# A decoder layer in float32 on one core: half-size weight buffers, the second FFN's weight sums added from DRAM to DRAM during the attention, seven sums kept on chip, token sums in the opening

## The chip, the cores and the metric

The kernel runs on one core of a Trainium2 chip. The time is the device time of one execution in microseconds (us); the number that counts is the median of several runs. A profile of one execution stands beside the times: it lists every instruction of the engines TensorE (PE, and PEld for its weight loads), VectorE (DVE), ScalarE (ACT), GpSimd (POOL) and SyncE (SP), and the DMA transfers.

## The reference

One decoder layer for 512 tokens of width 1024, in float32: a half-step SwiGLU FFN, a token mixer, and a second half-step FFN, each inside RMSNorms.

```python
x = x + 0.5 * rms_norm(swiglu(rms_norm(x, ffn1_pre), w_gate1, w_up1, w_down1), ffn1_post)
y = token_mixer(rms_norm(x, mix_pre), ...)     # sparse + dilated attention, gated, projected
x = x + rms_norm(y, mix_post)
x = x + 0.5 * rms_norm(swiglu(rms_norm(x, ffn2_pre), w_gate2, w_up2, w_down2), ffn2_post)
# swiglu(h, g, u, d) = (silu(h @ g) * (h @ u)) @ d,   d_ff = 2816
```

The mixer projects to queries, keys and values of two attentions. The first ("nsa": 8 heads, each with a selected and a window branch, so 16 head items, plus compressed keys) and the second ("dil": dilated windows, 12 heads) are weighed with gates and projected back.

## The kernel before

**Numbers.** Every float32 operand is split into a high part (ScalarE, a cast that rounds) and a low part (VectorE, the difference), in `split`, L102. A product is three matmuls: high x high, low x high, high x low (`mm3`, L124).

**FFN, gate and up.** The 2816 hidden rows are 11 pairs of 128-row blocks (even and odd). For each pair the gate and up weights are four blocks of 512 KB, by input half h and member f. The first two pairs (`PLAIN`) are computed plainly. The other nine pairs use a Winograd form of Strassen's scheme: seven half-width products P1 to P7 instead of eight, with sums of weights (VectorE, `prep`, L429) and sums of tokens T1 to T4 (`token_sums`, L510). Their order is P2, P6, P5, P7, the next pair's P1, P4, P3 (`todo`, L495), and the weights of a product are prepared two products ahead (`AHEAD`). The weights come through three buffers called raw of 1 MB, each holding one (pair, h), loaded by SP (`load`, L281): the first half of the next pair after P2 is prepared, the second after P7.

**Sums of activations.** After each pair, `sums` (L343) forms the sums that the down product needs. One (E) is split and stays; X, the odd block (O) and Y are stored to DRAM by SP (`sxdram`, `odram`, `ydram`) and read back in the down product, four reloads ahead (`STAGED`), into slots named SP.

**Sums of down weights (the table).** The down product uses the same seven-product form with half as many tokens. Four of its seven weight operands are sums of quarters of the down weight: T2, T4, T1, T3. GpSimd's DMA queue makes them, in both FFNs, beside the gate and up work (`weight_sums`, L308): per block of 256 KB it loads two quarters into SBUF slots named PT, adds others with an accumulating DMA (`accum_op`), and stores the sums into a DRAM tile `tdram`. The steps are put behind the work of given pairs by a list (`SUMS`, L34), with a one-column copy on GpSimd that waits for the pair (L363).

**FFN, down.** `ffn_down` (L556) runs seven products in the order B11, T2, T3, T1, B21, B22, T4. Each reads its weights in three loads of up to 1 MB through the raw buffers, and between them splits the reloaded X, O and Y.

**Opening.** `opening` (L1436) runs the first pair for the first FFN with an order of instructions written by hand on ScalarE, VectorE and TensorE. The normalisation is applied afterwards, by a row of factors (`row`, L1507), so the squares of x (L1495), the power on GpSimd (L1497), a diagonal (L1500) and a matmul with ones (L1506) make that row. After it x transposed is multiplied by its gain (L1510), and the token sums are formed from it after the first pair, on VectorE (L521). T4 is copied into the place of a part of the tokens before the first seven-product pair (L413 to L418).

**Attention.** In `nsa` (L1043) each of the 16 head items has its scores, its softmax, a scaling of the probabilities by GpSimd (L1008) and ScalarE (L1006), transposes (L1017) and the value product, the last three two items later (`LAG`). Pieces of the gate projection fill in between (`merge_unit`).

**Order.** Outside the opening a scheduler orders each engine's queue from the program's order and the dependencies; `issue_after` adds an order between two instructions of one engine. Each queue, SP's and GpSimd's DMA issues too, is first in, first out: an instruction that waits holds all behind it.

Of the kernel before, what the change touches and what calls it, by code (L numbers as in the profile page):

```python
# [12 lines left out]
F32 = mybir.dt.float32  # L13
F32R = mybir.dt.float32r
# [18 lines left out]
STAGED = 4  # L33
SUMS = [(0,), (1, 2)] + [(p + 1,) for p in range(2, 9)] + [(10, 11, 12), ()]  # L34
# [22 lines left out]
class Layer:  # L57
# [214 lines left out]
    def ffn(self, gu, wd, post, finish, xsrc, aside=None, opened=None):  # L272
# [5 lines left out]
        raws = {}  # L278
        later = {}

        def load(p, h):  # L281
            if (p, h) not in raws and p < NP:
                raws[p, h] = self.raw(gu[h, p].rearrange("p (f c) -> p f c", f=2), [2, D])

        def blk(p, h, f):
            return raws[p, h][:, f]
# [21 lines left out]
        def weight_sums(p):  # L308
# [3 lines left out]
            part = lambda q, e, h: wd[(2 * q + e) * P:(2 * q + e + 1) * P, h * S:(h + 1) * S]  # L312
# [12 lines left out]
            if one:  # L325
                put(self.tdram[p - 1][:, 0], later[p - 1][0])
            if two:
                put(self.tdram[p - 2][:, 1], later[p - 2][0])
            if new:
                for e in range(2):  # L330
                    put(self.tdram[p][:, 2 + e], r[e])
# [3 lines left out]
        E = []  # L335

# [6 lines left out]
        def sums(p, ev, od):  # L343

            h = slice(0, 256), slice(256, 512)
            x, y = self.slot("CB"), self.slot("ring")
# [5 lines left out]
            nc.sync.dma_start(self.sxdram[p], x)  # L352
# [5 lines left out]
        def extra(p):  # L358
            if p == 4 and aside:
                aside()  # L360
            if SUMS[p]:
                mark = self.sbt("mark", [P, 1])
                behind = nc.gpsimd.tensor_copy(mark, E[p][0][:, 0:1].bitcast(F32)).ins  # L363
                with self.tc.issue_after(behind):
                    for q in SUMS[p]:
                        weight_sums(q)

        banks = dict(opened["banks"]) if opened else {}
        if opened:
            raws.update(opened["raws"])  # L370
        else:
            ents = []
            for f in range(2):
                for h in range(2):
                    load(0, h)
                    w = entry(blk(0, h, f), len(ents) == 3)
                    ents.append(w)
# [11 lines left out]
        tops = None  # L389
        for p in range(PLAIN):  # L390
            acts = []
            for h in range(2):
                load(p + 1, h)
            for f in range(2):
                key = 2 * p + f
                if p:
                    ws = [None if (key, 0) in banks and h == 0 else entry(blk(p, h, f)) for h in range(2)]
# [11 lines left out]
            if p == 0:  # L409
                tops = self.token_sums(t_tags, opened)  # L410
            extra(p)
        t4 = tops["T4"]
        for m, v in enumerate((self.xht, self.xlt)):  # L413
            dst = v[:, 0:4, 256:512]
            if m == 0:
                nc.scalar.copy(dst, t4)
            else:
                nc.vector.tensor_sub(dst, t4, self.xht[:, 0:4, 256:512].bitcast(F32))  # L418
# [10 lines left out]
        def prep(p, name):  # L429
            st = state.setdefault(p, {})  # L430
            if name == "P1":
                load(p, 0)
                load(p, 1)
# [11 lines left out]
            elif name == "P7":  # L445
                src = blk(p, 0, 1)
                nc.vector.tensor_sub(src, blk(p, 0, 0), src)
# [57 lines left out]
        self.ffn_down(E, wd, post, finish, xsrc, opened)  # L505
# [4 lines left out]
    def token_sums(self, tags, opened):  # L510
# [4 lines left out]
        if opened:  # L515
            xt = opened["xt"]

        def diff(dst, a, b):
            if opened:
                for j in range(4):  # L520
                    nc.vector.tensor_sub(dst[:, j], xt[a[0] + j][:, a[1]], b[:, j] if not isinstance(b, tuple) else xt[b[0] + j][:, b[1]])  # L521
                return
# [10 lines left out]
        def keep(name, t):  # L533
            parts = [], []
            for m in range(2):
                w = [self.slot(tags.pop(0), F32R).rearrange("p (j c) -> p j c", j=2) for _ in range(2)]
                self.split(w[0], w[1], t[:, 2 * m:2 * m + 2])
# [1047 lines left out]
```

## Time and profile before

| what | us |
|---|---|
| median of 3 runs (lowest, highest) | 1189.32 (1188.61, 1190.68) |
| the profiled execution | 1193.05 |
| its span, first to last instruction | 1191.1 |

The stages as they lie in the span: opening and first FFN from 0 to about 375 us, the first attention's heads from about 430 to 555, the second attention and the projections to about 830, the second FFN from there to the end. In the profile a row of an engine list gives the start and length in us, engine, line, operation, operand shapes, and in brackets the idle time before it with what ended it. A row of the table of windows gives the busy time and the count of instructions of each engine, the granted TensorE clock as a share, the share in which the 16 DMA engines were busy, and GB/s.

### The profile page before, as it was taken

How to read it: one execution, taken by the hardware profiler on the slowest of the kernel's cores; microseconds unless marked ns; L12 is line 12 of the kernel's file. 1: busy time of each engine (PE TensorE's matmuls, PEld its weight loads, DVE VectorE, ACT ScalarE, POOL GpSimd, SP SyncE). 2: the span in 40 equal slices, each digit the busy share in tenths (PEclk: the TensorE clock that was granted, in tenths of full speed). 3: DMA queues.
4: the chain of work that ended last, by engine and by line, in shares of the span. 5: the costliest groups of instructions: out<-in, count | busy, mean ns of one | idle time of the engine just before them, and what ended most of it. 6: DMA issues, size and time to landing. Idle time of an engine off the chain costs nothing.

```text
span 1191.1 us, 18466 instructions
## 1 busy us (share of the span) xinstructions
PE 1138.5 (96%) x6863; PEld 1001.6 (84%) x6863; DVE 881.2 (74%) x1553; ACT 641.5 (54%) x1154; POOL 245.4 (21%) x350
## 2 busy tenths in 40 slices
PE   9899999978999999999999999999998999978997
PEld 7699999966877988778888898888898999976885
DVE  5789899957668779687444647966977898856675
ACT  5645455546455677686564625544443555535552
POOL 1143324230002032343000000001243333330001
PEclk9999999989999999999999999999998999998999
DMA  9598999999856462111224516473279998999863
GB/s 334 178 250 240 232 270 265 275 304 325 301 195 181 117 175 80 49 50 47 79 79 125 160 57 182 140 248 137 89 222 236 282 263 259 256 308 325 310 203 128
DMA packets 126859, 236.97 MB, mean 199 GB/s; under 512 B 22033, under 2 KB 51761, under 8 KB 121393
## 3 DMA queue, kind: packets, MB, share of 16 engines
q1 hardware_dynamic: 103392, 177.84, 45.4%
q0 software_dynamic: 23232, 57.69, 20.0%
q8 instruction: 54, 0.88, 0.3%
q14 instruction: 37, 0.30, 0.1%
q10 hardware_dynamic: 144, 0.26, 0.1%
HBM read 187.73 MB, written 48.02 MB: 198 GB/s over the span
## 4 chain that ended last, share of the span: by engine, by line
PE 52%; DVE 18%; DMA 13%; issue 10%; ACT 4%; POOL 1%; SPq 0%; DVEq 0%; POOLq 0%; ACTq 0%
PE pb_F L128 7%; PE pb_F L127 7%; PE pb_F L126 7%; DMA raw<-in_gu_dram 7%; DVE wlo L104 5%; PE pb_S L128 4%; PE pb_S L127 4%; PE pb_S L126 4%; PE pb_T L127 3%; PE pb_T L128 3%; PE pb_T L126 3%; DMA PT_s<-in_ffn_w_down_dram 3%; PE pb_V L1032 2%; DMA raw<-in_ffn_w_down_dram 1%; PE pb_T L1017 1%
## 5 line engine op out<-in xcount | busy, mean ns | idle before, releaser
L104 DVE TENSOR_TENSOR wlo<-raw,whi 128x1024 fp32r<-128x1024 f32 (+2 forms) x237 | 280.3, 1186 | 173.4 <-ACT whi L103 166.7
L103 ACT CAST whi<-raw 128x1024 fp32r<-128x1024 f32 (+2 forms) x237 | 241.1, 1018 | 268.1 <-PE pb_F L127 56.6
L126 PE MATMUL pb_F<-xh_t,whi 128*128 128x512 f32 (+1 forms) x440 | 156.7, 356 | 1.9 <-DVE Q_s L1242 1.1
L128 PE MATMUL pb_F<-xh_t,wlo 128*128 128x512 f32 (+1 forms) x440 | 155.7, 354 | 1.2 <-DVE wlo L104 1.2
L127 PE MATMUL pb_F<-xl_t,whi 128*128 128x512 f32 (+1 forms) x440 | 155.5, 353 | 0.0
L311 POOL DMA_DIRECT2D PT_s<-in_ffn_w_down_dram x88 | 78.4, 997 | 100.1 <-DMA PT_s<-in_ffn_w_down_dram 69.4
L126 PEld LDWEIGHTS pb_F<-xh_t,whi 128*128 128x128 f32 x440 | 82.9, 188 | 13.1 <-DVE Q_s L1242 1.3
L128 PEld LDWEIGHTS pb_F<-xh_t,wlo 128*128 128x128 f32 x440 | 82.9, 188 | 12.9 <-DVE wlo L104 2.2
L127 PEld LDWEIGHTS pb_F<-xl_t,whi 128*128 128x128 f32 x440 | 82.9, 188 | 11.0 <-issue 0.2
L128 PE MATMUL pb_S<-xh_t,wlo 128*128 128x256 f32 (+1 forms) x280 | 86.4, 309 | 4.5 <-DVE wlo L104 4.5
L126 PE MATMUL pb_S<-xh_t,whi 128*128 128x256 f32 (+1 forms) x280 | 86.6, 309 | 4.2 <-DVE V_s L482 3.8
L147 POOL TENSOR_TENSOR rs_t<-rs_t,mhalf_t 128x1 f32<-128x1 f32 x20 | 15.3, 763 | 358.4 <-DVE rs_t L143 358.4
L127 PE MATMUL pb_S<-xl_t,whi 128*128 128x256 f32 (+1 forms) x280 | 86.1, 307 | 0.0
L1008 POOL TENSOR_SCALAR SP_s<-SP_s,st_t 128x384 f32<-128x384 f32 (+2 forms) x48 | 47.8, 1012 | 103.9 <-DVE st_t L944 71.7
L126 PEld LDWEIGHTS pb_S<-xh_t,whi 128*128 128x128 f32 x280 | 55.0, 196 | 7.2 <-DVE V_s L482 4.0
L128 PEld LDWEIGHTS pb_S<-xh_t,wlo 128*128 128x128 f32 x280 | 54.9, 196 | 7.2 <-DVE wlo L104 5.0
L128 PE MATMUL pb_T<-xh_t,wlo 128*128 128x256 f32 x200 | 56.4, 282 | 1.1 <-DVE wlo L104 1.1
L127 PEld LDWEIGHTS pb_S<-xl_t,whi 128*128 128x128 f32 x280 | 55.0, 196 | 2.2
L126 PE MATMUL pb_T<-xh_t,whi 128*128 128x256 f32 x200 | 56.3, 282 | 0.0
L127 PE MATMUL pb_T<-xl_t,whi 128*128 128x256 f32 x200 | 56.1, 280 | 0.0
L103 ACT CAST whi<-tmp_t 128x1024 fp32r<-128x1024 f32 x36 | 37.6, 1048 | 21.1 <-issue 10.1
L128 PE MATMUL pb_S<-SP_s,wlo 128*128 128x256 f32 x160 | 45.4, 284 | 0.0
(799 smaller groups left out, 3322.3 us busy)
## 6 DMA issues: line engine op xcount, KB each, us to landing
raw<-in_gu_dram SPq DMA_DIRECT2D x42, 1024.0 KB, 7.2
PT_s<-in_ffn_w_down_dram POOLq DMA_DIRECT2D x132, 256.0 KB, 6.9
tdram<-PT_s POOLq DMA_DIRECT2D x88, 256.0 KB, 7.1
raw<-in_w_in_dram SPq DMA_DIRECT2D x18, 1024.0 KB, 5.5
raw<-tdram SPq DMA_DIRECT2D x16, 1024.0 KB, 7.4
raw<-in_ffn_w_down_dram SPq DMA_DIRECT2D x12, 1024.0 KB, 7.2
raw<-tdram SPq DMA_DIRECT2D x8, 768.0 KB, 6.7
odram<-W_s SPq DMA_DIRECT2D x22, 256.0 KB, 6.1
```

The costliest lines, as they stand in the source:

```text
L103: self.last_cast = self.nc.scalar.copy(dsthi, src).ins
L104: self.nc.vector.tensor_sub(dstlo, src, dsthi.bitcast(F32))
L126: mm(out, lhi, rhi, start=start, stop=False, skip_group_check=skip)
L127: mm(out, lhi, rlo, start=False, stop=False, skip_group_check=skip)
L128: mm(out, llo, rhi, start=False, stop=stop, skip_group_check=skip)
L147: nc.gpsimd.tensor_tensor(out=r, in0=v, in1=self.mhalf, op=OP.pow)
L311: add = lambda dst, src: put(dst, src, accum_op=OP.add)
L1008: nc.gpsimd.tensor_scalar(pp, pp, st[:, 1, t:t + 1], None, op0=OP.mult)
L1017: nc.tensor.transpose(b[:, o + (t - kk) * P:o + (t - kk + 1) * P], pt[pn][:, po + kk * P:po + (kk + 1) * P], self.ident)
L1032: self.nc.tensor.matmul(out[:, kk * P:S], v, pp, start=first and kk == 0 and pi == 0, stop=False, skip_group_check=True)
```

## The change

- **Weight buffers.** The three raw buffers are used as six halves of 512 KB. `ring_of` and `refill` load the blocks in their order of use; each half is refilled as soon as its block is used. P7's difference is formed while P6 is prepared. The weights lie in DRAM by blocks of 512 KB.
- **The first FFN's table** starts behind the row of the opening with two steps, and every later step comes one pair earlier; behind the pair of index 9 stand the steps 11 and 12, no longer 10.
- **The second FFN's table** is made in the first attention: `table_sums`, called for each of the 16 head items behind its scalings on GpSimd, copies and adds up to three blocks at a time from DRAM to DRAM; nothing passes SBUF. Its calls 0 to 13 hold 16 copies and 16 adds. Each FFN has its own `tdram`, and down weight and table lie in DRAM so that a partition's blocks are next to each other (a load's rows are 8 KB long).
- **Sums kept.** In the second FFN the X of the pairs from index 4 on (seven) stays in PT slots; it isn't stored and reloaded. Eight reloads are staged ahead instead of four.
- **Token sums.** In the first FFN they are formed in the opening, from x transposed, with the gain applied in the difference (`scaled_sums`); only four of the eight multiplications by the gain are left, ahead of the row. T4's split is in two halves.

The diff, cut to its core:

```diff
-STAGED = 4
-SUMS = [(0,), (1, 2)] + [(p + 1,) for p in range(2, 9)] + [(10, 11, 12), ()]
+STAGED = 8
+KEEP = 4
+SUMS = [(0, 1)] + [(p,) for p in range(2, 11)] + [(11, 12), ()]
...
+    def ring_of(self, gu, tiles, loaded):
+        self.order = [(h, p, f) for p in range(NF // 2) for f in range(2) for h in range(2)][loaded:]
+        self.blocks_of = {}
+        self.gu = gu
+        for t in tiles:
+            for f in range(2):
+                self.refill(t[:, f])
+
+    def refill(self, v):
+        if self.order:
+            key = self.order.pop(0)
+            self.nc.sync.dma_start(v, self.gu[key])
+            self.blocks_of[key] = v
...
-            x, y = self.slot("CB"), self.slot("ring")
+            x, y = self.slot("CB" if opened or p < KEEP else "PT"), self.slot("ring")
...
-            nc.sync.dma_start(self.sxdram[p], x)
+            if opened or p < KEEP:
+                nc.sync.dma_start(self.sxdram[p], x)
+            else:
+                kept[p] = x
...
+            if opened:
+                sums_behind(E[p][0][:, 0:1].bitcast(F32), SUMS[p + 1])
...
+            tops = opened["tops"]
+            sums_behind(row[:, 0:1], SUMS[0])
...
-                nc.vector.tensor_sub(src, blk(p, 0, 0), src)
...
-            if name == "P2":
-                load(p + 1, 0)
-            elif name == "P7":
-                load(p + 1, 1)
+            if name == "P6":
+                nc.vector.tensor_sub(blk(p, 0, 1), blk(p, 0, 0), blk(p, 0, 1))
+                self.refill(blk(p, 0, 0))
+            elif name in ("P7", "P4", "P3"):
+                self.refill(src)
...
+    def scaled_sums(self, tags, xt, g, out):
...
+        def diff(k, c, b):
+            t = new()
+            for j in range(4):
+                nc.vector.scalar_tensor_tensor(t[j // 2][:, j % 2], xt[k + j][:, c], g[:, k + j:k + j + 1], b(j),
+                                               op0=OP.mult, op1=OP.subtract)
+            return t
...
+        out["T3"] = self.keep_sum(tags, diff(4, hi, lambda j: xt[j][:, hi]))
+        t1 = less(lambda j: xt[j][:, hi], lambda j: xt[j][:, lo])
+        out["T1"] = self.keep_sum(tags, t1)
+        yield
+        t2 = diff(4, hi, of(t1))
+        out["T2"] = self.keep_sum(tags, t2)
+        out["T4"] = diff(4, lo, of(t2))
+        yield
...
             if m >= 0:
                 i, half, br = heads[m]
+                with self.tc.issue_after(self.last_pool):
+                    sums(m)
...
+    def table_sums(self, wd, td, call):
+        put = self.nc.gpsimd.dma_start
+        for b in range(0, NF // 2, 3):
+            q = slice(b, min(b + 3, NF // 2))
+            step = call - b
+            if step in (0, 1):
+                for i, e, h in ((2, 0, 1), (3, 1, 1), (0, 1, 1), (1, 1, 0))[2 * step:2 * step + 2]:
+                    put(td[i, :, q], wd[e, h, :, q])
+            elif step == 2:
+                put(td[2, :, q], wd[0, 0, :, q], accum_op=OP.add)
+                put(td[3, :, q], wd[0, 1, :, q], accum_op=OP.add)
+            elif step == 3:
+                put(td[0, :, q], td[2, :, q], accum_op=OP.add)
+            elif step == 4:
+                put(td[1, :, q], td[0, :, q], accum_op=OP.add)
...
             for t in range(NT):
                 if t == 2:
-                    w = self.wsplit(raws[1, 0][:, 0], [D])
+                    w = self.wsplit(third[:, 0], [D])
+                    self.refill(third[:, 0])
+                    for k in range(4):
+                        nc.scalar.mul(xt[k], xt[k], gcol[:, k:k + 1])
                 nc.scalar.activation(xn[t], xn[t], AF.Square, scale=D ** -0.5, accum_out=ss[:, t:t + 1])
+            tops = {}
+            sums = self.scaled_sums(list(T_TAGS), xt, gcol, tops)
+            next(sums)
             nc.vector.tensor_scalar(ss, ss, EPS, None, op0=OP.add)
             nc.gpsimd.tensor_tensor(out=rs, in0=ss, in1=self.mhalf.to_broadcast([P, NT]), op=OP.pow)
+            next(sums)
...
-            for k in range(KT):
-                nc.scalar.mul(xt[k], xt[k], gcol[:, k:k + 1])
...
-        self.tdram = self.tc.dram_tile([NF // 2, P, 4, S], F32, name="tdram")
+        td = [self.tc.dram_tile([4, P, NP, S], F32, name=f"tdram{i}") for i in range(2)]
...
+        self.mixer(*boundary(a["mix_post"][0], a["ffn2_pre"][0], self.x2dram, AFTER_MIX),
+                   lambda m: self.table_sums(a["d2"], td[1], m))
```

More of the change, by code (lines that the diff above doesn't have):

```diff
@@ L388, in ffn, with entered @@
                         mms(ents[2 * f + h], h, n, banks[f, n], 2 * P, S)
-        tops = None
+        def entered(p, h, f):
+            w = entry(blk(p, h, f))
+            self.refill(blk(p, h, f))
+            return w
         for p in range(PLAIN):
             acts = []
-            for h in range(2):
-                load(p + 1, h)
             for f in range(2):
@@ L396, in ffn @@
                 if p:
-                    ws = [None if (key, 0) in banks and h == 0 else entry(blk(p, h, f)) for h in range(2)]
+                    ws = [None if (key, 0) in banks and h == 0 else entered(p, h, f) for h in range(2)]
                     bs = [banks[key, n] if (key, n) in banks else self.bank() for n in range(2)]
@@ L408, in ffn @@
             sums(p, *acts)
-            if p == 0:
-                tops = self.token_sums(t_tags, opened)
+            if p == 0 and not opened:
+                tops = self.token_sums(t_tags)
             extra(p)
         t4 = tops["T4"]
[L413 to L418, printed above, removed]
+        for m in range(len(t4)):
+            n = 4 // len(t4)
+            c = slice(m * n, m * n + n), slice(256, 512)
+            self.split(self.xht[:, c[0], c[1]], self.xlt[:, c[0], c[1]], t4[m])
         tops.update(T4=self.xop(0, 256), B11=self.xop(0, 0), B21=self.xop(4, 0), B22=self.xop(4, 256))
@@ L504, in ffn, with keep_sum, token_sums @@
             finished(p, name)
-        self.ffn_down(E, wd, post, finish, xsrc, opened)
+        self.ffn_down(E, kept, wd, td, post, finish, xsrc, opened)
     def xop(self, k, c):
         return [lambda j, v=v: v[k + j][:, c:c + 256] for v in (self.xh, self.xl)]
-    def token_sums(self, tags, opened):
+    def keep_sum(self, tags, parts):
+        out = [], []
+        for t in parts:
+            w = [self.slot(tags.pop(0), F32R).rearrange("p (j c) -> p j c", j=2) for _ in range(2)]
+            self.split(w[0], w[1], t)
+            for o, v in zip(out, w):
+                o.append(v)
+        return [lambda j, v=v: v[j // 2][:, j % 2] for v in out]
+    def token_sums(self, tags):
         nc = self.nc
@@ L533, in keep @@
         def keep(name, t):
[L534 to L537, printed above, removed]
-                for o, v in zip(parts, w):
-                    o.append(v)
-            out[name] = [lambda j, v=v: v[j // 2][:, j % 2] for v in parts]
+            out[name] = self.keep_sum(tags, [t[:, 0:2], t[:, 2:4]])
         new = lambda: self.sbt("tmp", [P, 4, 256], bufs=2)
@@ L568, in ffn_down @@
         parts = {"X": [], "O": [], "Y": []}
-        srcs = [("X", i) for i in range(NP)] + [("O", i) for i in range(NP)] + [("Y", i) for i in range((NP + 1) // 2)]
+        srcs = [("X", i) for i in range(NP) if i not in kept] + [("O", i) for i in range(NP)] + [("Y", i) for i in range((NP + 1) // 2)]
         staged = {}
@@ L1440, in opening @@
         xt = [self.slot("x") for _ in range(KT)]
-        raw = [self.pool.tile([P, 4, S], F32, name="raw", tag="raw", bufs=3) for _ in range(2)]
+        raw = [self.raw_tile([4, S]) for _ in range(2)]
         gcol = self.sbt("gcol", [P, KT])
@@ L1456, in opening, with rows @@
         xn = []
-        raws = {}
-        for t in range(NT):
+        def rows(t):
             xn.append(self.sbt("tmp", [P, D], bufs=2))
             nc.sync.dma_start(xn[t], a["x"][0][t * P:(t + 1) * P])
-            if t % 2:
-                raws[1, t // 2] = self.raw(gu[t // 2, 1].rearrange("p (f c) -> p f c", f=2), [2, D])
+        self.ring_of(gu, (), 4)
+        third = self.raw_tile([2, D])
+        for t in range(2):
+            rows(t)
+            self.refill(third[:, t])
         ones = self.sbt("onesq", [P, P])
@@ L1487, in opening @@
                 nc.vector.tensor_sub(lo, src, hi.bitcast(F32))
+                if k % 2:
+                    self.refill(raw[k // 4].rearrange("p (a b) s -> p a (b s)", a=2)[:, (k // 2) % 2])
+                    if k < 4:
+                        rows(2 + k // 2)
                 for i, (l, r) in enumerate(((hi, xh[k]), (hi, xl[k]), (lo, xh[k]))):
```

95 lines of the change are left out of this document (49 added, 46 removed).

## The prediction

> **What bounds the kernel now.** I read the page first, then the table of stages (busy times in chosen windows), then the order-of-time lists of the engines around each hole, then the chain that ended last. The page gives the frame:
>
> ```profile
> span 1191.1 us, 18466 instructions
> ...
> PE 1138.5 (96%) x6863; PEld 1001.6 (84%) x6863; DVE 881.2 (74%) x1553; ACT 641.5 (54%) x1154; POOL 245.4 (21%) x350
> ...
> q1 hardware_dynamic: 103392, 177.84, 45.4%
> q0 software_dynamic: 23232, 57.69, 20.0%
> ```
>
> TensorE is the bound: 52.6 us idle in 1191.1. Idle time is not the whole loss, because matmuls after a hole run at a lower granted clock. So I count matmuls per window; the columns are busy time and (count) per engine, then granted clock, DMA share and GB/s.
>
> ```profile
> core 0: us, PE busy (x) PEld busy (x) DVE busy (x) ACT busy (x) POOL busy (x), PEclk, DMA share, GB/s
> 54.30:64.20 9.90, 5.75 (x29) 5.55 (x28) 9.87 (x15) 2.06 (x3) 4.08 (x7) 0.66 0.91 213
> 75.00:150.00 75.00, 71.67 (x581) 70.69 (x581) 66.61 (x92) 36.84 (x53) 25.32 (x38) 0.98 0.90 246
> 150.00:225.00 75.00, 75.00 (x635) 75.00 (x635) 71.72 (x102) 40.98 (x57) 25.68 (x39) 1.00 0.91 268
> 250.00:300.00 50.00, 39.75 (x149) 30.09 (x148) 32.26 (x44) 26.54 (x40) 6.15 (x10) 0.90 1.00 326
> 300.00:350.00 50.00, 49.93 (x217) 40.26 (x216) 30.87 (x36) 25.82 (x36) 0.00 (x0) 1.00 0.76 260
> 438.00:545.00 107.00, 106.09 (x592) 84.58 (x591) 88.12 (x274) 81.38 (x202) 42.84 (x48) 1.00 0.21 62
> ...
> 905.00:925.00 20.00, 15.84 (x110) 15.34 (x109) 13.39 (x18) 7.04 (x11) 5.97 (x9) 0.83 0.87 249
> ...
> 975.00:1050.00 75.00, 74.47 (x627) 74.06 (x626) 66.92 (x88) 39.44 (x58) 26.64 (x43) 1.00 0.95 266
> ...
> 1064.00:1100.00 36.00, 25.18 (x85) 18.62 (x84) 20.54 (x29) 18.38 (x28) 4.89 (x7) 0.81 1.00 324
> ```
>
> 150 to 225 is the undisturbed rate of the half-width products (635 in 75 us, 0.1181 us each), 300 to 350 that of the down product (217 in 50 us, 0.2304 each). What the other windows lose against these: 54.3 to 64.2: 9.9 - 29 x 0.1181 = 6.5 us; 75 to 150: 75 - 581 x 0.1181 = 6.4; 250 to 300: 50 - 149 x 0.2304 = 15.7; 905 to 925: 7.0; 975 to 1050: 0.9; 1064 to 1100: 16.4. Together 52.9 us, all in the two FFNs, and all but the first where the DMA share is 0.87 to 1.01. The attention (438 to 545) loses nothing and has the DMA engines at 0.21. The losses end on these transfers and queue entries:
>
> ```profile
> 132.86 8.34 DMA raw<-in_gu_dram
> ...
> 145.77 1.14 DVE raw L447
> ...
> 275.07 8.87 DMA PT_s<-in_ffn_w_down_dram
> ...
> 1051.39 17.24 DMA raw<-in_ffn_w_down_dram
> ...
> 1072.67 8.24 DMA sxdram<-CB_s
> ```
>
> ```profile
> 900.64 10.71 DMA raw<-in_gu_dram
> ```
>
> ```profile
> 259.41 0.79 PE L126 MATMUL pb_F<-whi,KB_s 128*128 128x512 f32 x1 [5.87 <-ACT whi L103]
> ```
>
> ```profile
> 1063.15 0.37 SPq L87 DMA_DIRECT2D raw<-tdram  x1
> ...
> 1083.55 0.37 SPq L87 DMA_DIRECT2D raw<-tdram  x1
> ```
>
> A down-weight load took 17.24 us. In the second down product, SP's queue went 20 us from one table load to the next (1063.15, 1083.55), because between them stands the reload of the last spilled X sum, which waits for its store (8.24 us from 1072.67).
>
> **Prices of the DMA work.**
>
> ```profile
> L311 POOL DMA_DIRECT2D PT_s<-in_ffn_w_down_dram x88 | 78.4, 997 | 100.1 <-DMA PT_s<-in_ffn_w_down_dram 69.4
> ...
> PT_s<-in_ffn_w_down_dram POOLq DMA_DIRECT2D x132, 256.0 KB, 6.9
> tdram<-PT_s POOLq DMA_DIRECT2D x88, 256.0 KB, 7.1
> raw<-in_w_in_dram SPq DMA_DIRECT2D x18, 1024.0 KB, 5.5
> ```
>
> q1 moves 177.84 MB in 45.4% of 1191.1 us: 0.329 MB/us, so a plain block of 256 KB (0.262 MB) takes 0.80 us of all 16 engines. q0 carries nothing but the table sums, 220 blocks, in 20.0%: 238 us. 132 of these are plain (105 us at 0.80), so the 88 adds (L311) take the other 133: 1.51 us each, nearly twice a plain one. One FFN's table (44 adds, 66 plain) costs 119 us of the DMA engines.
>
> **The change part by part.**
>
> *Token sums to the opening.* Now they stand on VectorE between the two plain pairs and the products:
>
> ```profile
> 40.30 2.77 DVE L521 TENSOR_TENSOR tmp_t<-x_s 128x256 f32<-128x256 f32 x8 [0.19 <-ACT x_s L1510]
> ...
> 45.93 0.68 DVE L104 TENSOR_TENSOR SP_s<-tmp_t,SP_s 128x512 fp32r<-128x512 f32 x1
> ...
> 55.96 1.21 DVE L418 TENSOR_TENSOR xl_t<-tmp_t,xh_t 128x1024 fp32r<-128x1024 f32 x1
> ...
> 57.43 1.22 DVE L104 TENSOR_TENSOR wlo<-raw,whi 128x1024 fp32r<-128x1024 f32 x1
> ```
>
> ```profile
> 58.70 0.58 PE L128 MATMUL pb_S<-xh_t,wlo 128*128 128x256 f32 x1 [4.15 <-DVE wlo L104]
> ```
>
> P1's weight split (57.43) comes last of a backlog, and TensorE waits 4.15 us and then runs at a granted clock of 0.66 in the window: the 6.5 us. The change takes 16 differences (2.77 / 8 = 0.35 each, 5.5 us) and six splits (0.68, 4.1 us) out of 40 to 54. The sum T4 is ready early, so its cast waits only for TensorE; L418 remains, as two halves of the same elements. I take the whole 6.5 as gone. The opening pays:
>
> ```profile
> 25.00 1.06 ACT L1495 ACTIVATE tmp_t<-tmp_t 128x1024 f32<-128x1024 f32 x1 [2.33 <-DMA tmp_t<-in_x_dram]
> ```
>
> ```profile
> 26.18 0.17 DVE L1496 TENSOR_SCALAR ssum_t<-ssum_t 128x4 f32<-128x4 f32 x1 [3.68 <-ACT tmp_t L1495]
> ...
> 36.60 1.23 DVE L104 TENSOR_TENSOR wlo<-raw,whi 128x1024 fp32r<-128x1024 f32 x1 [5.09 <-PE pb_V L1506]
> ```
>
> ```profile
> 35.55 1.02 PE L1506 MATMUL pb_V<-W_s,onesq_t 128*128 128x512 f32 x2
> ```
>
> T3's and T1's casts queue on ScalarE behind the last Square (26.1). In the written order four splits (2.7 us), four differences (1.4) and a cast's wait come ahead of L1496, which moves from 26.2 to about 30.7; then eight differences (2.8), two splits (1.4) and a cast come ahead of the diagonal. L1506 can start at 36 to 38 instead of 35.55. VectorE's 3.68 and 5.09 us of idle time cover the rest. I charge 2 us (0 to 4): net 4.5 gained (1 to 6.5).
>
> *Half-size buffers.* Bytes stay. A block's successor is asked for as soon as that block is used (P6, P7, P4, P3), nearly a pair (about 20 us) ahead of its use, where now the second 1 MB load of a pair goes out at P7, four products (4 x 24 x 0.118 = 11 us) ahead of it. The loads that end the chain take 8.34 and 10.71 us, so the longer lead covers them. P7's difference (1.14 us, L447) now stands in front of P5's split; preparation runs two products (5.7 us) ahead, which hides it; uncovered it would cost 1.1 us in each of nine pairs. I take 4.5 of the 6.4 us in the first FFN (0 to 6.4): there the DMA share stays at 0.91 and VectorE is 71.72 of 75 us busy.
>
> *First FFN's table one pair earlier.* Behind the last products now stand three steps of the table (10, 11, 12), then two (11, 12). Step 10 has 4 adds and 6 plain blocks: 4 x 1.51 + 6 x 0.80 = 10.8 us of DMA less in 250 to 300, paid from the 37 to 60 us stretch. On the other side STAGED 8 puts four more 256 KB reloads (3.2 us) ahead of the down loads, and the last two of the first product's three loads go into tiles free only at P3. Net 7.6 of the 15.7 us, and the down loads now read whole 8 KB rows; I take 9 (2 to 15).
>
> *Second FFN.* Its table leaves: 119 us of DMA time out of about 220 us that are 0.83 to 1.01 full, leaving a share near 0.45. The 10.71 us load goes back towards the 5.5 us of a quiet 1 MB load. I take 7.0 and 0.9 whole: 8 (6 to 8). Seven of the eleven X sums stay in SBUF, so the reload that blocked SP is gone, with 14 blocks. Of the 16.4 us I take 14 (9 to 16.4): the first product still has loads that wait for P3's tile.
>
> *The table in the attention.* 44 plain blocks and 44 adds, up to three blocks in a transfer: 35 + 66 = 101 us of DMA; with the 0.21 x 107 = 22 us already there, 123 us in the 107 us of the 14 calls. So the transfers lag, by up to 16 us at the end. Each add waits on POOL for the landing of the step before. Behind it on POOL stand the next head's probability scalings (L1008) and the key memsets of the dilated part; the transposes on TensorE (L1017) wait for the scalings. How much lag is free:
>
> ```profile
> 482.33 2.72 POOL L1008 TENSOR_SCALAR SP_s<-SP_s,st_t 128x384 f32<-128x384 f32 x3 [0.76 <-DVE st_t L944]
> ...
> 542.43 2.73 POOL L1008 TENSOR_SCALAR SP_s<-SP_s,st_t 128x384 f32<-128x384 f32 x3 [1.09 <-DVE st_t L944]
> ```
>
> ```profile
> 508.54 0.90 PE pb_T L1017 x8
> ...
> 550.18 0.76 PE pb_T L1017 x7
> ```
>
> In mid-attention the scalings are done 23 us before their transposes (485.1, 508.5), at the end 5 (545.2, 550.2). Issuing costs POOL about 1 us each (997 ns in the L311 row), two or three per head, against 42.84 of 107 us busy: free. I charge half of the lag, 8 us (0, as the middle heads' spare covers it all, to 20: the whole lag and two weight loads late by 2 us). An add between two DRAM places is not in the trace; its bounds are the plain block, 0.80, and twice the SBUF add, 3.0 (it may read both operands from DRAM); I take 1.51, the nearest row.
>
> The Trainium skill (DMA: Bandwidth & Descriptors, Anatomy of one DMA) fits a POOL-issued transfer as 2.0 us plus bytes / 436e3, with no extra term for adding. By it, an estimate, the 88 blocks move in 53 us and the attention pays nothing. The q0 row disagrees: 57.69 MB in 238 us is 0.242 MB/us.
>
> **Sum.** 4.5 + 4.5 + 9 + 8 + 14 - 8 = 32 us. The profiled execution took 1193.05 us (span 1191.1 and 1.95 around it): 1161. It stands 3.7 above the 1189.32 median of the three runs: 1157.
>
> **Rivals.**
> 1. *The adds are slow in DRAM; slower than before.* At x us a block, the calls need 22 + 35 + 44x us of DMA. Gains elsewhere are 40 us; with 8 us of lag absorbed, the sign turns at 107 + 48 = 155, x = 2.2. At x = 3.0 it is 189: 82 - 8 - 40 = 34 slower, 1223. For: 123 is already over 107. Against: source and destination streams both exist in the SBUF add at 1.51. Chance 0.07.
> 2. *DMA keeps the pace in the first FFN.* Its bytes are the same and only move by a pair; then its 13.5 us of stalls stay and the gain is 18.5: 1171. For: share 0.90 to 1.00 from 75 to 300. Chance 0.2.
> 3. *Adds cost no more than plain blocks, or the spare covers the lag.* 88 x 0.80 + 22 = 92 us fit in 107; nothing is charged: 1149; with the first FFN's holes nearly closed too (6.4 + 15.7 instead of 13.5), 1141. Against: the q0 row. The Trainium skill's fit quoted above (DMA: Bandwidth & Descriptors) would end here too. Chance 0.2.
> 4. *The transfers aren't issued where they are written.* The queue order is a scheduler's; issued after the attention they meet the dilated part: 1149 to 1160. Chance 0.03.
>
> **Numbers.** The forecast's own chance is 0.5, its range 1149 to 1166. The range with rivals 2 and 3 is 1139 to 1175; rival 1 is left out. A measurement of this kernel tells about 0.2% (2.4 us) from no change. Slower: rival 1 and a little, 0.08; same 0.03; faster 0.89.
>
> **What would show it.** Right: no PE hole near 54 or 905, q0 busy in 438 to 545, no tdram stores from POOL after 855, DMA share near 0.45 there, windows of the second down product at 0.23 us a matmul. Wrong: holes at L1017 <- POOL in the attention (rival 1), holes still at 250 to 300 (rival 2), L1506 later than 40, or a second FFN that stalls with idle DMA engines.

## The result, and the profile after

| | kernel before | kernel after |
|---|---|---|
| median, us (lowest, highest; runs) | 1190.0 (1188.61, 1195.91; 4) | 1151.45 (1148.51, 1154.33; 4) |
| the profiled execution, us (span) | 1193.05 (1191.1) | 1151.49 (1149.7) |

The ratio is 0.9667, 95% interval 0.9626 to 0.9708: 38.6 us faster (the two profiled executions lie 41.4 us apart in span). The forecast of 1157 was 0.9728 of its 1189.32; the chip gave about 7 us more.

The page of after, its span, engine and queue lines:

```profile
span 1149.7 us, 18444 instructions
...
PE 1122.6 (98%) x6863; PEld 990.7 (86%) x6863; DVE 882.7 (77%) x1554; ACT 641.1 (56%) x1151; POOL 184.0 (16%) x263
...
q1 hardware_dynamic: 93088, 174.18, 45.1%
q0 software_dynamic: 16224, 51.91, 18.0%
```

TensorE is idle for 27.1 us instead of 52.6. It has the same 6863 matmuls, and its busy time fell by 15.9 us too: the mean granted clock rose from 0.981 to 0.995, and 1138.5 x 0.981 and 1122.6 x 0.995 are both 1117. Busy time after a hole is stretched by a lower clock, so a closed hole gives back more than its own length. The table of windows of after, at the places that the prediction counted (the columns are the same):

```profile
54.30:64.20 9.90, 9.90 (x84) 9.81 (x83) 7.42 (x11) 5.51 (x7) 3.98 (x8) 1.00 0.96 291
75.00:100.00 25.00, 23.05 (x181) 22.82 (x180) 20.64 (x30) 11.79 (x17) 12.30 (x18) 0.93 0.97 282
100.00:150.00 50.00, 50.00 (x423) 50.00 (x422) 49.00 (x71) 27.10 (x39) 19.64 (x27) 1.00 0.95 279
...
250.00:300.00 50.00, 50.00 (x214) 40.34 (x213) 38.58 (x50) 30.86 (x44) 0.56 (x1) 0.99 0.92 341
300.00:350.00 50.00, 48.27 (x213) 38.29 (x212) 36.13 (x50) 29.10 (x49) 5.66 (x7) 1.00 0.61 198
425.00:500.00 75.00, 73.75 (x411) 58.73 (x409) 61.61 (x189) 55.07 (x137) 41.18 (x48) 1.00 1.04 283
500.00:525.00 25.00, 23.91 (x132) 18.73 (x133) 20.34 (x65) 18.37 (x46) 15.49 (x20) 1.00 0.95 230
825.00:1025.00 200.00, 200.00 (x1595) 195.31 (x1594) 178.29 (x226) 103.56 (x144) 0.00 (x0) 1.00 0.39 125
1040.00:1100.00 60.00, 59.58 (x255) 47.49 (x254) 45.87 (x59) 36.38 (x50) 0.00 (x0) 1.00 0.72 251
```

Read the counts first. 54.3 to 64.2 holds 84 matmuls where it held 29: full rate (9.9 / 0.1181 = 84). 100 to 150 is at full rate (423), though the DMA share is still 0.95. 250 to 300 holds 214 instead of 149, at 0.92. The second FFN's gate and up stage has no idle TensorE at all, with the DMA engines at 0.39. The 60 us from 1040 hold 255 of the 260 that 0.2304 us each allow. The price stands at 425 to 525: the DMA engines are full, and TensorE loses a little.

Four places still cost something. In the opening the row's matmul (L1506 before, L1590 now) starts 1.83 us after the matmul ahead of it, where 0.23 is usual: 1.6 us lost; at 94 us there is a new hole. Both in the PE list, and the second also in the lists of DVE and of SP:

```profile
36.38 0.40 PE L129 MATMUL pb_F<-xh_t,wlo 128*128 128x512 f32 x1
38.21 1.12 PE L1590 MATMUL pb_V<-W_s,onesq_t 128*128 128x512 f32 x2 [1.44 <-DVE W_s L1584]
...
91.80 0.28 PE L128 MATMUL pb_V<-xl_t,whi 128*128 128x256 f32 x1
94.03 0.55 PE L129 MATMUL pb_V<-xh_t,wlo 128*128 128x256 f32 x1 [1.95 <-DVE wlo L105]
```

```profile
91.62 1.23 DVE L461 TENSOR_TENSOR tmp_t<-raw 128x1024 f32<-128x1024 f32 x1 [4.29 <-DMA raw<-in_gu_dram]
```

```profile
85.28 0.33 SPq L285 DMA_DIRECT2D raw<-in_gu_dram  x1
```

A weight block asked for at 85.28 lands 6.3 us later, in a stretch where the DMA share is 0.97 and the first table steps run. VectorE had been ready for it at 87.33 (91.62 - 4.29), 2.0 us after it was asked for. In the first down product a shorter hole stays (it was 5.87 us before):

```profile
246.44 0.50 PE L127 MATMUL pb_F<-whi,KB_s 128*128 128x512 f32 x1 [1.53 <-ACT whi L104]
```

And in the attention GpSimd waits for its own transfers; some rows of its list:

```profile
467.33 0.87 POOL L1181 DMA_DIRECT2D tdram<-tdram  x1 [3.87 <-DMA tdram<-in_d_dram]
...
494.69 0.87 POOL L1181 DMA_DIRECT2D tdram<-tdram  x1 [2.13 <-DMA tdram<-in_d_dram]
...
518.92 0.87 POOL L1181 DMA_DIRECT2D tdram<-tdram  x1 [3.25 <-DMA tdram<-in_d_dram]
```

To sort the time by stage I take the start of six instructions in both traces: the first matmul of the first down product (before 242.01, after 233.39), one of the last of the first FFN's down products (374.06, 354.25), the last head's transposes (555.65, 538.27), the first matmul of the second FFN's gate and up work (822.57, 805.73), and the first and one of the last matmuls of the second down product (1053.75, 1027.72 and 1183.75, 1141.85). A stage's gain is the difference of its lengths. The second attention and the projections, and the end of the kernel, are not in the table: they differ from before by about 0.5 us at most, except that the second attention and the projections are 2.3 us shorter in adds_twice. This table has it for each profile, with every kernel's median and its ratio to the kernel before on the same chip:

| kernel | median us | ratio (95%) | opening, gate/up 1 | down 1 | attention | gate/up 2 | down 2 |
|---|---|---|---|---|---|---|---|
| after | 1151.45 | 0.9667 (0.9626, 0.9708) | 8.6 | 11.2 | -2.4 | 9.2 | 15.9 |
| after_again | 1154.28 | 0.9666 (0.9638, 0.9693) | 6.5 | 12.4 | -3.9 | 9.2 | 16.0 |
| u_table | 1162.56 | 0.9762 (0.9738, 0.9785) | 8.1 | 11.6 | 0.0 | 6.7 | 3.1 |
| u_keep | 1154.66 | 0.9693 (0.9676, 0.9710) | 6.6 | 12.4 | -5.6 | 9.1 | 14.4 |
| u_late | 1151.21 | 0.9657 (0.9620, 0.9694) | 6.0 | 13.7 | -3.5 | 9.2 | 16.2 |
| u_table_late | 1165.16 | 0.9772 (0.9739, 0.9805) | 8.5 | 11.3 | 0.0 | 3.4 | 1.7 |
| u_sums | 1158.21 | 0.9727 (0.9709, 0.9744) | 10.8 | 4.7 | -4.9 | 9.2 | 16.7 |
| u_tokens | 1156.95 | 0.9711 (0.9693, 0.9729) | 4.4 | 8.6 | -4.2 | 9.6 | 16.0 |
| adds_plain | 1148.0 | 0.9625 (0.9594, 0.9656) | 9.0 | 11.4 | -0.2 | 9.2 | 16.3 |
| adds_twice | 1210.89 | 1.0144 (1.0104, 1.0184) | 6.9 | 13.3 | -67.3 | 9.2 | 15.9 |
| spread | 1150.87 | 0.9647 (0.9617, 0.9676) | 7.4 | 13.4 | -3.8 | 9.2 | 16.5 |
| row_first | 1154.57 | 0.9668 (0.9640, 0.9697) | 5.0 | 14.1 | -5.1 | 9.2 | 15.7 |
| best | 1155.35 | 0.9681 (0.9653, 0.9710) | 5.4 | 11.8 | -3.9 | 9.1 | 16.3 |

Gate/up 1 and down 1 trade with each other between profiles of the same code; their sum is steadier (19.0 to 20.8 where the first FFN is untouched: after, after_again, u_table, u_keep, adds_plain, adds_twice, spread). The trace shows the trade: after waits 1.95 us at 94 us and 1.53 in the first down product, after_again 2.57 us at 96 us and not over 0.9 us in the down product.

### The profile page after: what moved, and what is told of

It reads as the page before. It is cut to its first block, busy times and chain, and to the rows that moved or that the text cites. A ratio compares the mean times of both kernels' runs of the same rounds, so it can differ in the third digit from the quotient of the medians.

```text
span 1149.7 us, 18444 instructions
## 1 busy us (share of the span) xinstructions
PE 1122.6 (98%) x6863; PEld 990.7 (86%) x6863; DVE 882.7 (77%) x1554; ACT 641.1 (56%) x1151; POOL 184.0 (16%) x263
## 4 chain that ended last, share of the span: by engine, by line
PE 70%; issue 10%; DVE 9%; DMA 6%; ACT 3%; POOL 2%; SPq 0%; DVEq 0%; POOLq 0%; ACTq 0%
PE pb_F L129 8%; PE pb_F L128 8%; PE pb_F L127 8%; PE pb_S L127 6%; PE pb_S L128 6%; PE pb_S L129 6%; PE pb_T L128 5%; PE pb_T L129 5%; PE pb_T L127 5%; DVE wlo L105 2%; PE pb_V L127 2%; PE pb_V L129 2%; PE pb_V L128 2%; DMA tdram<-in_d_dram 2%; DMA PT_s<-in_d_dram 1%
## 5 line engine op out<-in xcount | busy, mean ns | idle before, releaser
L127 PE MATMUL pb_S<-xh_t,whi 128*128 128x256 f32 (+1 forms) x280 | 84.2, 301 | 0.0
L129 PE MATMUL pb_S<-xh_t,wlo 128*128 128x256 f32 (+1 forms) x280 | 83.8, 300 | 0.0
L127 PEld LDWEIGHTS pb_S<-xh_t,whi 128*128 128x128 f32 x280 | 52.7, 188 | 2.5 <-ACT V_s L496 0.2
L128 PEld LDWEIGHTS pb_S<-xl_t,whi 128*128 128x128 f32 x280 | 52.7, 188 | 2.3
L105 DVE TENSOR_TENSOR wlo<-tmp_t,whi 128x1024 fp32r<-128x1024 f32 x36 | 43.8, 1217 | 3.3 <-ACT whi L104 3.2
L127 PE MATMUL pb_S<-SP_s,whi 128*128 128x256 f32 x160 | 45.3, 283 | 0.0
```

The lines of the kernel that those rows point to most:

```text
L105: self.nc.vector.tensor_sub(dstlo, src, dsthi.bitcast(F32))
L127: mm(out, lhi, rhi, start=start, stop=False, skip_group_check=skip)
L128: mm(out, lhi, rlo, start=False, stop=False, skip_group_check=skip)
L129: mm(out, llo, rhi, start=False, stop=stop, skip_group_check=skip)
```

## The experiments

**What the table's move is worth: u_table and u_keep.** Both store and reload all eleven X sums; u_table also makes the second FFN's table beside its own gate and up work again.

```diff
-KEEP = 4
+KEEP = 11
# u_table alone:
-            if opened:
-                sums_behind(E[p][0][:, 0:1].bitcast(F32), SUMS[p + 1])
+            sums_behind(E[p][0][:, 0:1].bitcast(F32), SUMS[p + 1] if opened else OLD[p])
...
-                   lambda m: self.table_sums(a["d2"], td[1], m))
+                   lambda m: None)
```

Expected of u_table:

> The changed kernel with the second FFN's table made beside its gate and up work again, by the steps of the list of before, and with all eleven X sums stored and reloaded, since the table needs the PT slots. Theory (the table's 119 us of DMA time are what the second FFN waited for): the second FFN loses again what it won, 9 us in its gate and up part and about 16 in its down part, and the attention gets 2.4 back, so about 1174 us, with the DMA share above 0.8 in the second FFN's gate and up part. Rival (the half-size buffers and the longer rows did it, and the place of the table matters little): at most 1157.

and of u_keep:

> The changed kernel with all eleven X sums of the second FFN stored and reloaded (no sum kept). Theory: with the table gone, the store of the last X lands in about 3 us and its reload holds SP's queue no longer, so the kept sums are worth 0 to 3 us: 1151 to 1155. Rival (the reload of the last X on SP's queue was the cause of the second down product's holes, whatever the DMA load): 8 us or more, 1160, with holes of over 3 us in the second down product.

u_table gave 1162.56, between the two theories: with the table back and no sum kept, 9.8 of the second FFN's 25 us stay. Its windows in the second FFN, and the hole in the down part:

```profile
825.00:1025.00 200.00, 198.91 (x1576) 193.38 (x1575) 174.95 (x223) 101.80 (x142) 76.85 (x108) 1.00 0.87 253
...
1040.00:1100.00 60.00, 53.12 (x205) 41.23 (x206) 41.95 (x56) 36.23 (x52) 3.45 (x5) 0.91 0.93 335
```

```profile
1044.38 0.79 PE L128 MATMUL pb_F<-whi,KB_s 128*128 128x512 f32 x1 [5.26 <-ACT whi L105]
```

With the table back the DMA share is 0.87 and 0.93 instead of 0.39 and 0.72, a 5.26 us hole opens, and the same 60 us hold 205 matmuls instead of 255. In the gate and up work it matters less: 6.7 of the 9.2 us stay, with the DMA engines busy. So against u_keep the move alone brings 14.4 - 3.1 = 11.3 us in the down part and 2.4 in gate and up, and costs what the attention shows. The kept sums are worth 15.9 - 14.4 = 1.5 us in the down part; the ratios of u_keep and after differ by 0.0026 with intervals that overlap, so the kernels' times alone don't tell them apart.

**The longer lead: u_late and u_table_late.** The calls that refill the halves are moved to where a block would be asked for four products ahead, as before; the buffers stay half-size. u_table_late is u_table with the same edit.

```diff
-                self.refill(blk(p, 0, 0))
+                freed.append(blk(p, 0, 0))
             elif name in ("P7", "P4", "P3"):
-                self.refill(src)
+                freed.append(src)
+            elif name in ("P1", "P2") and p > PLAIN:
+                for _ in range(2):
+                    self.refill(freed.pop(0))
```

> The changed kernel with its half-size buffers, but a freed half is refilled later: two at the preparation of P1 and two at that of P2, so that every weight block is asked for four products ahead of its use, as before the change. Theory (the longer lead of the half-size buffers covers loads that queue behind the table in the first FFN; in the second FFN, whose DMA engines are then mostly idle, it does nothing): the first FFN's gate and up part loses 4 to 6 us, the second's at most 1: 1156. Rival (the lead is worth nothing, the order of the table and the token sums did it): within 1 us.

> Both: the second FFN's table made beside its gate and up work again (no X sum kept), and the late refills. With the table alone back, the second FFN's gate and up part still won 6.6 of 9.1 us. Theory now (either the lead or the table's removal closes the hole there, each alone is enough): with both undone the hole comes back, and the second FFN's gate and up part loses 6 to 9 us against the kernel with the table alone back; with the first FFN's 4 to 6, 1174. Rival (the order of SP's queue or the block-wise layout closed it): the second FFN's gate and up part as with the table alone, within 2 us.

u_late loses nothing: 1151.21, the same 9.2 us in the second FFN's gate and up work, and 19.7 in the first FFN. But the edit did not move the loads. In u_late each goes out at the same point of the sequence of matmuls as in after, within 12 matmuls (1.4 us), and after_again differs from after by as much. The block to look at is the last one of a pair: a sum on VectorE (L461; L462 in u_late, L439 before) waits for it. For the pair of index 9 in the second FFN, the load on SP and the sum on VectorE, in after:

```profile
981.07 0.33 SPq L285 DMA_DIRECT2D raw<-in_gu_dram  x1
...
984.90 1.23 DVE L461 TENSOR_TENSOR tmp_t<-raw 128x1024 f32<-128x1024 f32 x1 [1.45 <-DMA raw<-in_gu_dram]
```

in u_late:

```profile
981.72 0.33 SPq L285 DMA_DIRECT2D raw<-in_gu_dram  x1
...
985.70 1.23 DVE L462 TENSOR_TENSOR tmp_t<-raw 128x1024 f32<-128x1024 f32 x1 [1.51 <-DMA raw<-in_gu_dram]
```

and before, where the load is the second 1 MB half of the pair of index 8:

```profile
986.29 0.33 SPq L87 DMA_DIRECT2D raw<-in_gu_dram  x1
...
994.01 1.22 DVE L439 TENSOR_TENSOR tmp_t<-raw 128x1024 f32<-128x1024 f32 x1 [2.63 <-DMA raw<-in_gu_dram]
```

Without its wait the sum would have started 2.4 us after the load was asked for in after (984.90 - 1.45 - 981.07), 2.5 in u_late and 5.1 before. Over all pairs but the first FFN's first seven-product pair this lead is 2.0 to 4.0 us in after, 2.0 to 4.3 in u_late and 3.5 to 5.7 before. So these two runs don't test the lead, and for this block there was no longer lead to take away. u_table_late has the same leads as u_table in the second FFN (2.4 to 3.3 us); its profile keeps 3.4 us in gate/up 2 instead of 6.7, but the two ratios differ by 0.0010 with intervals that overlap, and what makes the profiles differ is open. What did change for every load is its size: in the rows above 512 KB were there 3.8 us after the request, 1 MB after 7.7. That the smaller loads brought the gate and up work's gain is not shown.

**The first FFN: u_sums and u_tokens.** u_sums puts the first table's steps back behind their old pairs; u_tokens forms the token sums after the first pair again.

```diff
# u_sums
-SUMS = [(0, 1)] + [(p,) for p in range(2, 11)] + [(11, 12), ()]
+SUMS = [(), (0,), (1, 2)] + [(p + 1,) for p in range(2, 9)] + [(10, 11, 12), ()]
# u_tokens
-            if p == 0 and not opened:
-                tops = self.token_sums(t_tags)
+            if p == 0:
+                tops = self.token_sums(t_tags, opened)
...
-            sums = self.scaled_sums(list(T_TAGS), xt, gcol, tops)
-            next(sums)
```

> The changed kernel with the first FFN's table by the list of before (nothing behind the row, three steps behind the pair of index 9). Theory (step 10's 10.8 us of DMA at the end of the pairs are what the first down product waits for): about 8 of the 11 us gained there go, 1159, with a hole of over 4 us near the third load of the first down product. Rival (the 8 KB rows of the down loads and the earlier loads did it): 0 to 2 us, 1152.

> The changed kernel with the token sums formed after the first pair again, from x multiplied by its gain behind the row. Theory: the hole of 4 us with the lower clock behind it comes back before the first products (6.5 us), and the wait of 1.8 us for the row's matmul in the opening goes: 4 to 5 us slower, 1156. Rival (the hole came from the DMA load of the first FFN, not from VectorE's backlog): within 1 us.

u_sums' windows, and its hole in the down part:

```profile
75.00:100.00 25.00, 24.40 (x203) 23.98 (x202) 21.99 (x33) 12.60 (x18) 9.47 (x13) 1.00 0.97 258
...
250.00:300.00 50.00, 47.05 (x197) 37.00 (x196) 37.94 (x50) 30.50 (x44) 2.60 (x4) 0.98 0.97 351
```

```profile
247.59 0.80 PE L127 MATMUL pb_F<-whi,KB_s 128*128 128x512 f32 x1 [4.88 <-ACT whi L104]
```

A wait of 4.88 us is back, and the down part keeps 4.7 of 11.2 us. But 75 to 100 holds 203 matmuls, 22 more than after, and the hole at 94 us is gone. The size of this other side is uncertain: the profiles with the first FFN untouched hold 169 to 197 matmuls there, and u_tokens, which has the earlier table but comes to this place later, holds 211. Over the whole first FFN the order is worth 19.8 - 15.5 = 4.3 us in the profiles, and 0.0060 x 1190 = 7.1 by the ratios. u_tokens shows the old hole again (29 matmuls, as before):

```profile
54.30:64.20 9.90, 5.75 (x29) 5.46 (x28) 9.87 (x16) 1.66 (x2) 4.24 (x8) 0.72 0.79 224
```

It keeps 13.0 us of the first FFN's 19.8: the sums in the opening are worth 6.8 net there, and 0.0044 x 1190 = 5.2 by the ratios.

**What an add costs: adds_plain and adds_twice.** The second FFN's table alone is touched.

```diff
# adds_plain
-                put(td[0, :, q], td[2, :, q], accum_op=OP.add)
+                put(td[0, :, q], td[2, :, q])
# adds_twice
-                put(td[0, :, q], td[2, :, q], accum_op=OP.add)
+                for _ in range(2):
+                    put(td[0, :, q], td[2, :, q], accum_op=OP.add)
# and so for each of the four kinds of add
```

> The changed kernel with every add of the second FFN's table in the attention replaced by a plain copy of the same size: the second FFN's table then holds no sums. Theory (an add costs about two copies of DMA time, and the attention loses 2.4 to 5.7 us because the transfers lag and POOL waits): the DMA share in the attention falls from 1.0 to about 0.75, POOL's waits for landings go, the attention is back within 1 us of before, 1148. Rival (the attention loses by GpSimd's issuing or by the weight loads, not by the adds' lag): the attention stays 2 us or more behind.

> The changed kernel with every add of the second FFN's table issued twice, so that the second FFN's sums are wrong by the doubled term. By the formula of the prediction's first rival, with the durations measured since (copies 27 us, adds 56, doubled 112, other transfers 22, against 107 us of heads), the lag is over 50 us; if it passes to the attention, less about 20 us of spare, this is 30 to 35 us slower than the changed kernel, 1183. Rival (POOL's and the heads' spare takes nearly all, as it took 20 of the 22 us of lag expected with single adds): at most 12 us, 1163.

In 400 to 640 us q0 carries the second FFN's table and nothing else. Its line there (packets, MB, share) in after, adds_plain and adds_twice:

```profile
q0 software_dynamic: 4608, 23.07, 37.8%
```

```profile
q0 software_dynamic: 4608, 23.07, 27.4%
```

```profile
q0 software_dynamic: 6912, 34.61, 63.7%
```

and adds_twice's waits of PE from 420 to 620:

```profile
PE pb_T L1067 <- POOL SP_s L1058: 42.8, 16, 9.0
```

Of these 240 us the table takes 0.378 x 240 = 90.7 in after, 65.8 in adds_plain and 152.9 in adds_twice. The 88 copies of adds_plain cost 65.8 / 88 = 0.75 us each. 44 adds turned into copies save 24.9 us, so an add costs 0.57 more than a copy, 1.32; 44 adds more cost 62.2, or 1.41 each. adds_plain takes the attention's cost to 0.2 us, with the DMA share at 0.92 from 425 to 500 (1.04 in after) and 0.50 from 500 to 525 (0.95). adds_twice shows rival 1's mechanism: GpSimd's list has, for each head, a wait for the step before ahead of the scalings,

```profile
455.59 0.81 POOL L1183 DMA_DIRECT2D tdram<-tdram  x1 [8.07 <-DMA tdram<-tdram]
456.13 0.81 POOL L1176 DMA_DIRECT2D tdram<-in_d_dram  x1
456.70 2.99 POOL L1058 TENSOR_SCALAR SP_s<-SP_s,st_t 128x384 f32<-128x384 f32 x3
```

and the transposes wait 42.8 us for these. The 62 us of added transfer made the heads 65 us longer than in after, of which the second attention and the projections make up 3: in this run, with the spare used up, added DMA time passed to the end one for one. I had expected 1183; the expectation put the adds at 56 us where they take 58 to 62, and let 20 us of lag be absorbed.

**Two attempts to win more: spread, row_first, best.** With after_again as their measure on the same chip:

> The kernel after the change, unaltered, as the measure for the other three on the same chip: about 1151 us, a ratio of 0.967 to the kernel before.

spread puts the table's steps behind every second head, and the later ones into the second attention:

```diff
-                with self.tc.issue_after(self.last_pool):
-                    sums(m)
+                if m % 2 == 0:
+                    with self.tc.issue_after(self.last_pool):
+                        sums(m // 2)
# in dil, behind the key memsets
+                with self.tc.issue_after(self.last_pool2):
+                    sums(8 + 2 * g + j)
```

> The steps of the second FFN's table stand behind every second head of the first attention and go on behind the key memsets of the second (dilated) attention; nothing else is changed. Theory: the attention pays because the adds and copies (DMA share about 1.0 from 425 to 500) hold GpSimd's queue, and with it the scalings of the probabilities; at half the density they finish before the next ones are issued. The last head's transposes then come 2 to 5 us earlier, nothing is lost later, and the time is about 1148, 2 to 5 us under the unaltered kernel. Rival: the cost is that of issuing on GpSimd and only moves to the dilated part, which has GpSimd work of its own: 1151, no difference.

1150.87 against 1154.28: the intervals overlap, and the stages don't support the theory, because the attention lost 3.8 us, no less than after_again's 3.9. The windows show what happened:

```profile
425.00:500.00 75.00, 74.26 (x415) 59.53 (x415) 60.74 (x188) 56.78 (x141) 37.23 (x42) 1.00 0.66 189
500.00:525.00 25.00, 24.89 (x140) 19.50 (x138) 22.55 (x70) 19.31 (x51) 8.92 (x14) 1.00 0.63 155
525.00:550.00 25.00, 22.28 (x117) 17.50 (x117) 14.88 (x28) 11.21 (x21) 12.61 (x17) 1.00 1.00 255
```

Up to 525 the share is 0.66 and the matmuls are a little more than in after (415 against 411, 140 against 132). Then, on GpSimd:

```profile
512.18 1.33 POOL L1177 DMA_DIRECT2D tdram<-in_d_dram  x2
514.30 0.23 POOL L1204 IOTA W_s<- 128x128 int32 x1 [0.80 <-DVE st_t L817]
522.10 0.86 POOL L1179 DMA_DIRECT2D tdram<-in_d_dram  x1 [7.56 <-PE pb_T L1067]
522.69 3.25 POOL L1058 TENSOR_SCALAR SP_s<-SP_s,st_t 128x384 f32<-128x384 f32 x3
```

GpSimd starts nothing between 514.5 and 522.1, with an add next in its queue and the scalings of the last heads behind it; these then come in a bunch, and TensorE is idle for about 2.7 us from 525 to 550, where after has no idle time. The trace names a transpose as what ended that wait; two copies issued at 512.2 were under way as well, and which of the two held the add was not tried. The rival (the cost moves to the dilated part) isn't shown either; the second attention's 575 to 600 us and after lose nothing.

row_first writes the sum, the power and the diagonal of the row of factors ahead of the splits of T3 and T1:

```diff
-        out["T3"] = self.keep_sum(tags, diff(4, hi, lambda j: xt[j][:, hi]))
+        t3 = diff(4, hi, lambda j: xt[j][:, hi])
...
+        yield
+        out["T3"] = self.keep_sum(tags, t3)
         out["T1"] = self.keep_sum(tags, t1)
-        yield
# the next step of these sums (next(sums)) is called behind the diagonal instead of ahead of it
```

> In the opening the sum and the power of the row of factors, and its diagonal, are written ahead of the splits of T3 and T1; nothing else is changed. Theory: the 1.8 us that TensorE waits for the diagonal in the opening (36.4 to 38.2 us) come from the splits that stand ahead of it on VectorE, so they go: about 1149 to 1150. Rival: the splits are then late for the first seven-product pair, and the loss moves to 54 to 64 us: 1151 or more.

1154.57, no difference from after_again. The row's matmul came in time (35.57 instead of 38.21), and the loss moved to where the rival had put it, but not for the rival's reason. Its PE list, ahead of the third half-width product, and a row of its DVE list:

```profile
35.57 1.02 PE L1591 MATMUL pb_V<-W_s,onesq_t 128*128 128x512 f32 x2
...
62.66 0.39 PE L127 MATMUL pb_S<-SP_s,whi 128*128 128x256 f32 x1 [3.51 <-ACT V_s L496]
```

```profile
53.67 0.43 DVE L363 TENSOR_TENSOR CB_s<-ring_s 128x256 f32<-128x256 f32 x1 [4.43 <-DMA sxdram<-CB_s]
```

The copy that TensorE waits for (L496) stands on ScalarE behind work that needs VectorE, and VectorE had waited 4.43 us for the store of the first pair's X, issued at 44.53, to write the second pair's X into its slot. In after the same row starts at 49.23 without a wait. The row of factors also starts the first table steps: GpSimd issues the first adds at 41.25 here, ahead of that store, and at 45.20 in after, behind it (store at 44.18). That these adds delayed the store fits the order, but was not tried.

best has both edits:

> Both of the two last edits together: the table's steps over both attentions, and the row of factors ahead of two splits. If both theories hold, their gains add: about 1146 (1144 to 1150). If only the spreading helps, 1148; if neither, 1151.

1155.35: neither gain is there. In best, with the same edit of the row, VectorE waits 2.87 us for that store and TensorE does not stop (83 matmuls from 54.3 to 64.2), but it waits 2.69 us at 97 us. No full kernel here beats the changed one beyond the intervals.

## Why the prediction came out

- **The bound and the place of the gains** were right. All of the gain lies in the two FFNs, in the stages that were counted, and TensorE is still the bound.
- **Opening, buffers and first table** (4.5 + 4.5 + 9 = 18) gave 19.8, in other shares than forecast, so that their sum came out is in part luck. The token sums brought 6.8 (what u_tokens lost), the whole hole at 54 us having gone for 1.6 us lost before the row's matmul (2 were charged). The prediction's own row has a DMA share of 0.91 in that window, like the others; that VectorE's backlog and not the DMA load made the hole is what u_tokens shows. The table's order brought 4.3 of the 9 (7.1 by the ratios). What is left, about 9 us, is due to the buffers, the 8 KB rows and the deeper staging together; one by one they were not tried.
- **The half-size buffers' reason fell.** The prediction said that a block is asked for nearly a pair (about 20 us) ahead, and that this lead covers the 8 and 10 us loads. The last block of a pair, the one that VectorE waits for, was asked for 2.0 to 4.0 us ahead, less than the 3.5 to 5.7 before. So the 4.5 us had no right reason; what the half-size loads bring by themselves is open.
- **The first table's early start** is paid, but not where I said (37 to 60 us). The trace has it at 94 us, where a weight block lands late beside the first steps; u_sums, with a later table, has no hole there and 22 matmuls more, 22 x 0.1181 = 2.6 us, a number that spreads by as much between profiles of the same code.
- **Second FFN** (8 + 14 = 22) gave 25, of which 9.8 stay with the table back and no sum kept (u_table); these are not separated. DMA share 0.39 and 0.72, no TensorE hole of note, as forecast. The part of SP's blocked queue was smaller than it sounded: the kept sums bring 1.5 us, the table's absence 11.3.
- **The table in the attention** is the term that was mis-sized: -8 forecast, -2.4 to -5.6 in the seven profiles with this attention code; the five that lost 3.9 or more show a granted clock of 0.93 or 0.94 from 525 to 550, the other two 1.00, so a fall of the clock is part of the difference. The mechanism was right: GpSimd waits for landings, and the scalings behind it come late. The lag was too large: copies cost 0.75 instead of 0.80, adds 1.32 to 1.41 instead of 1.51, so with the 91 us of the table in after the demand is 22 + 91 = 113 us where I had 123: 6 us over the heads' 107, not 16. The Trainium skill (DMA: Bandwidth & Descriptors, Anatomy of one DMA) has no term for adding in its fit; by that fit adds_plain would have changed nothing. It took 24.9 us off q0, so the trace disagrees.
- **Rivals.** Rival 1 is what adds_twice made of the kernel: at 2 x 1.41 = 2.8 us for an add it is slower than before (ratio 1.0144, 1.0104 to 1.0184), and the forecast's turning point of 2.2 stands between. Rival 2 (1171) fell: 100 to 150 and 250 to 300 run at full rate or close to it with DMA shares of 0.95 and 0.92. Rival 3 (1149 or 1141) is close in time, but for another reason: adds do cost more than plain blocks, and the attention pays less for it than I charged. Rival 4 fell, the transfers are issued between the scalings.

## What to carry to other kernels

Move bulk transfers to a stage whose DMA engines are idle, but work out the demand against that stage's length with the price of an add kept apart from that of a copy: with the demand 6 us over the stage's length the cost was 2 to 6 us, and in the run far beyond it every added microsecond came through. A transfer that waits for another one also blocks what stands behind it in its queue, so see what compute work shares the queue. When an experiment takes a part of a change out, look in its trace whether the thing moved at all: u_late's calls were moved and its loads were not, and its time alone would have been read as a result.

## What the runs showed of the hardware

- An accumulating DMA from DRAM to DRAM costs the DMA engines 1.32 to 1.41 us for 256 KB, a plain copy 0.75: nearly twice, as into SBUF (1.51 against 0.80).
- Full DMA engines do not by themselves stall TensorE: at shares of 0.92 to 0.95 it ran at full rate or close to it (423 of 423 and 214 of 217 matmuls in 50 us), where before 0.90 to 1.00 came with holes.
- The length of a wait alone did not tell when the clock falls. After the 1.95 us wait at 94.03 in after it fell at once; after row_first's 3.51 us wait (to 62.66) matmuls ran at full rate for another 1.4 us and then at half. The rows of 3.4 us ahead of the fall and behind it, in after and in row_first:

```profile
90.70:94.10 3.40, 1.45 (x13) 1.24 (x12) 2.48 (x3) 1.05 (x1) 1.58 (x3) 1.00 0.76 266
94.10:97.50 3.40, 3.40 (x16) 3.40 (x17) 3.40 (x5) 0.29 (x1) 2.57 (x4) 0.50 0.80 172
```

```profile
60.70:64.10 3.40, 1.44 (x12) 1.45 (x13) 2.40 (x5) 2.60 (x4) 1.39 (x3) 1.00 1.02 263
64.10:67.50 3.40, 3.40 (x19) 3.40 (x18) 3.20 (x5) 1.43 (x3) 1.68 (x3) 0.50 1.05 275
```

In both, TensorE was busy for 1.4 of the 3.4 us ahead of the fall, and the low clock lasted 3.4 us. The Trainium skill (TensorE: Matmul & The Clock Gate, The HAM clock gate) lets the clock fall after an idle window of about 3.4 us; here a window that was idle for 2 of its 3.4 us was enough.
